# Transposing three quarters of the residual stream with DMA transposes in a two-layer decoder trunk

## The chip, the core and the metric

The kernel runs on one core of a Trainium2 chip. The engines that matter are TensorE (PE for matmuls, PEld for weight loads), VectorE (DVE), ScalarE (ACT) and SyncE (SP), which issues most of the DMAs. Each engine runs its own instruction list in order; semaphores tie the lists together. The metric is the device time of one execution in microseconds (us), as the median of several runs.

## The reference

Two pre-norm layers on a sequence of 256 tokens of width 2048, float32. Each layer has a mixing part (sparse attention and stick-breaking attention) and a SwiGLU part, both added to the residual stream `h`:

```python
def reference(x, positions, ...):
    h = x
    for layer in range(DEPTH):                       # DEPTH = 2
        xn = rms_norm(h, norm_mix[layer])
        h = h + hybrid_mixer(xn, ..., w_in[layer], ..., w_out[layer])
        xn = rms_norm(h, norm_ffn[layer])
        h = h + swiglu(xn, w_gate[layer], w_up[layer], w_down[layer])
    return rms_norm(h, norm_final)

def swiglu(xn, w_gate, w_up, w_down):                # inner width 5632
    return (jax.nn.silu(xn @ w_gate) * (xn @ w_up)) @ w_down
```

## The kernel before

**Precision.** Every large product is done in float32 as three passes of a reduced format: a number is split into `hi` and `lo`, and a product is hi·hi + hi·lo + lo·hi. Activations are split into `xh`/`xl` (or `ah`/`al` inside the SwiGLU part), weights into `hi`/`lo`.

**Weight items.** All weights are streamed in items of 512 KB (2 slices of 128 rows by 512 columns). `load_next` (L155) issues the load on SP into one of 5 `raw` buffers; `split_next` makes `hi` by a copy on ACT (L166) and `lo` by a subtraction on DVE (L167), each in one of 4 buffers; `mm` (L409) then issues 12 matmuls of 512 columns per item: two slices, three passes, two token tiles. `prefetch` keeps the split 3 items ahead of the matmuls and the loads 5 items ahead of the splits. A split can only start when the item four places earlier has released its `hi` buffer.

**Order around the items.** Everything else is written as Python generators. Before each item the main loop does `step(active)`, which advances every generator to its next `yield`, then `prefetch`, then `mm`. So a `yield` is one item of delay, and what a generator emits stands in each engine's list between two splits. The engines do not reorder: an instruction of a generator that waits on ACT holds up the splits behind it.

**Transposing the activations.** Matmuls need the activations with the feature on the partition. The residual stream `h` has the token there. `xt_block` transposes a quarter of `h` (512 features, 2 token tiles) by 8 PE transposes into PSUM (L374, tiles `tps`), multiplies by the norm's gain on DVE (L376, `scr`), copies to `xh` on ACT (L381) and subtracts to `xl` on DVE (L384). `xt_gen` wraps that in a generator. There are three places where `h` is transposed in the steady part: before the SwiGLU part of both layers (during the last column block `o3` of the output projection, items o0 to o3) and before the second layer's mixing part (during the last pass over `w_down`, blocks d0 to d3). Quarter 3 of `h` is final only when the last block is done, so its transposes stand right behind it.

**h_add and d_add** add a finished block to `h` on DVE (L864, L950), and a step later square it on ACT (L347) for the next norm; the last one finishes the norm.

**The gated chain.** Inside the SwiGLU part, `gated` transposes silu(gate)·up, 512 features at a time, without PE: ACT separates the float32 values into two planes of 16-bit halves (`pl`, L923), one DMA transpose moves both planes into `plt` (L926, issued on ACT's queue), ACT interleaves the planes again into `sT` (L934, four instructions), and ACT and DVE split the result into `ah` and `al` (L938, L939). It takes nine steps from the product to `ah`. There are 11 such chunks in each layer, consumed by `w_down` in two groups of 6 and 5 chunks. The first `w_down` block of a group starts right after the group's last chunk is multiplied, and reaches that chunk after 10 items (first group) or 8 items (second).

Of the kernel before, what the change touches and what calls it, by code (L numbers as in the profile page):

```python
# [7 lines left out]
F32 = mybir.dt.float32  # L8
# [114 lines left out]
def trunk(ctx: ExitStack, tc: tile.TileContext, x, positions, cst, gT, gfin, bgate, posT, w2, ws, out):  # L123
# [58 lines left out]
    def spawn(g):  # L182
        active.append(g)
# [204 lines left out]
    def tmp512(name="scr"):  # L388
        return tmpp.tile([P, 512], F32, tag="scr", name=name, bufs=3)

    def xt_gen(X, c, srcs, g, ready=None):
        if ready is not None:
            while ready not in flags:
                yield
        xt_alloc(X, c)
        xt_block(X, c, srcs, g)
        yield
# [43 lines left out]
    for l in range(DEPTH):  # L441
        g_mix, g_grp, g_ffn = gt[:, 3 * l, :], gt[:, 3 * l + 1, :], gt[:, 3 * l + 2, :]
        flags.clear()
        with ExitStack() as actx:
# [357 lines left out]
            def sb_driver(b):  # L802
                yield from wait_for("nsa", f"sq{b}", f"sk{b}")
                yield from pipeline([sb_unit(b, 0, [0, 1, 2, 3]), sb_unit(b, 1, [0, 1]), sb_unit(b, 1, [2, 3])], 2)

            spawn(prep())
            spawn(nsa_driver())
            spawn(sb_driver(0))
# [2 lines left out]

            ocmp = {}
            accs = None
            XO = new_x()
            while seq[pos][1].mat in ("w_in", "w_cmp_k1", "w_cmp_v1"):
                it = seq[pos][1]
                if l == 0 and pos < 6:
# [7 lines left out]
                if it.mat == "w_in":  # L825
                    for kt in it.kts:
                        while X[kt // 4] is None:
                            step(active)
                    if it.first:
                        accs = [acc(), acc()]  # L830
                    mm(pos, accs, lambda kt: X[kt // 4])
                    if it.last:
                        nm = it.name
                        if nm in ("ck", "cv"):
                            spawn(c_chunk(nm, accs))
                        elif nm == "v" or nm[:2] == "sv":
                            spawn(v_chunk(nm, accs))
                        else:
                            spawn(qk_chunk(nm, accs))
                    if it.name == "sv1" and it.kts[-1] in (3, 7, 11):  # L840
                        c = it.kts[-1] // 4
                        spawn(xt_gen(XO, c, lambda t, c=c: on[c][:, t], g_grp, f"on{c}"))
# [33 lines left out]
            while seq[pos][1].mat == "w_out":  # L876
# [5 lines left out]
                if XO[it.kts[0] // 4] is None:  # L882
                    while f"on{it.kts[0] // 4}" not in flags:
                        step(active)
                    need(XO, it.kts[0] // 4)
                    step(active)
                    step(active)
                mm(pos, accs[it.name], lambda kt: XO[kt // 4])
                c = int(it.name[1])
                if it.last:  # L890
                    spawn(h_add(accs[it.name], c, norm))
                if c == 3 and it.kts[-1] in (1, 5, 9, 15):
                    q = it.kts[-1] // 4
                    spawn(xt_gen(X, q, lambda t, q=q: h[:, t, quad(q)], g_ffn, f"h{q}"))
                parts.pop(pos)
                pos += 1

# [1 line left out]
        with ExitStack() as fctx:  # L899
# [14 lines left out]
            def gated(c, accs):  # L914
# [3 lines left out]
                    s = sil[c, t]  # L918
                    V.scalar_tensor_tensor(s, accs[t], r[:, t:t + 1], s, op0=OP.mult, op1=OP.mult)  # L919
                yield  # L920
                pl = fp.tile([P, 2, 2, 512], U16, tag="pl", name="pl", bufs=1)
                for t in range(2):
                    A.activation(pl[:, t], sil[c, t].bitcast(U16).rearrange("p (n b) -> p b n", b=2), AF.Copy)  # L923
                    yield
                pt = fp.tile([P, 2, 2, 512], U16, tag="plt", name="plt", bufs=1)
                nc.scalar.dma_start(pt.rearrange("p t b (a s) -> p (t b a) s", a=4),  # L926
                                    pl.rearrange("p t b n -> p (t b n)"), transpose=True)
                for _ in range(4):
                    yield
                f = fp.tile([P, 4, S], F32, tag="sT", name="sT", bufs=1)  # L930
                fv = f.rearrange("p a s -> p (a s)").bitcast(U16).rearrange("p (a t s b) -> p t b a s", a=4, t=2, b=2)
                for t in range(2):
                    for b in range(2):
                        A.activation(fv[:, t, b], pt[:, t, b].rearrange("p (a s) -> p a s", a=4), AF.Copy)  # L934
                    yield
# [3 lines left out]
                V.tensor_tensor(al, f, ah.bitcast(F32), op=OP.subtract)  # L939
                yield  # L940
                act[c] = (ah, al)

# [37 lines left out]
            while pos < (end_at if last else len(seq)) and seq[pos][1].mat in ("w_gate", "w_up", "w_down"):  # L980
# [10 lines left out]
                if it.last:  # L991
                    c = int(it.name[1:])
                    if it.mat == "w_down":
                        end = it.k1 == KFF
                        spawn(d_add(accs, c, end, norm))
                        if end and not last:
                            spawn(xt_gen(X, c, lambda t, c=c: h[:, t, quad(c)], gt[:, 3 * (l + 1), :], f"d{c}"))
                    else:
                        spawn(silu(c, accs) if it.mat == "w_gate" else gated(c, accs))
                parts.pop(pos)  # L1000
# [95 lines left out]
```

## Time and profile before

| what | value |
|---|---|
| median of 3 runs | 2296.75 us (2296.72 to 2298.61) |
| the profiled execution | 2295.14 us, of it 2293.4 us from its first to its last instruction |
| PE busy | 2269.5 us (99%) |
| DVE busy | 1322.7 us (58%) |
| ACT busy | 1176.6 us (51%) |
| weight loads, queue of SP (q1) | 426.58 MB, 58.4% of the 16 DMA engines |
| DMA transposes, queue of ACT (q10) | 11.54 MB, 3.1% |

Busy time of PE counts each matmul from its start to a modelled end; matmuls overlap, so the starts in the timeline tell what one costs. In the timeline a row is a run of equal instructions: start, time from the first start to the last end, engine, line, operation, tiles, shape, count and, in brackets, the idle time of the engine before it and what ended it.

### The profile page before, as it was taken

The numbers are of one execution on the slowest core, as the hardware profiler recorded it, in microseconds if no ns is written. First come the engines' busy times: TensorE is split into PE (matmuls) and PEld (weight loads), VectorE is DVE, ScalarE is ACT, GpSimd is POOL, SyncE is SP. The second block draws the span as 40 slices with busy tenths as digits, with TensorE's granted clock in tenths as the row PEclk, the third lists the DMA queues.
The fourth block names the chain that finished last, engine by engine and source line by source line (L and its number), as shares of the span: only waits on it lengthen the run. The fifth ranks groups of instructions, "written<-read, shape, count | busy, mean of one in ns | idle before, by whom it ended". The sixth has DMA issues, their size and how long they took to land. (4 is left out here: it accounts for less than half of the span.)

```text
span 2293.4 us, 28108 instructions
## 1 busy us (share of the span) xinstructions
PE 2269.5 (99%) x10666; PEld 1888.1 (82%) x10666; DVE 1322.7 (58%) x1744; ACT 1176.6 (51%) x1515; POOL 28.7 (1%) x59
## 2 busy tenths in 40 slices
PE   8999999999999999999999999999999999999998
PEld 7888888888888888887888888888888888888876
DVE  6766776655545444555567667765545554445554
ACT  6645554555554345555455455545555543455543
POOL 5000000000000000000000000000000000000000
PEclk9999999999999999999999999999999999999999
DMA  7854446567677667776567434456666665566663
GB/s 252 274 174 129 124 153 199 180 204 208 201 208 203 193 193 204 209 203 191 178 215 254 147 129 143 157 186 206 213 197 210 201 203 193 195 209 202 202 193 137
DMA packets 164584, 439.98 MB, mean 192 GB/s; under 512 B 59184, under 2 KB 59600, under 8 KB 164320
## 3 DMA queue, kind: packets, MB, share of 16 engines
q1 hardware_dynamic: 118464, 426.58, 58.4%
q10 hardware_dynamic: 45760, 11.54, 3.1%
q8 instruction: 83, 1.36, 0.2%
q14 instruction: 53, 0.43, 0.1%
q0 software_dynamic: 224, 0.07, 0.0%
HBM read 424.50 MB, written 2.10 MB: 186 GB/s over the span
## 5 line engine op out<-in xcount | busy, mean ns | idle before, releaser
L167 DVE TENSOR_TENSOR lo<-raw,hi 128x1024 fp32r<-128x1024 f32 (+1 forms) x798 | 969.4, 1220 | 829.3 <-ACT hi L166 821.4
L166 ACT ACTIVATE hi<-raw 128x1024 fp32r<-128x1024 f32 (+1 forms) x798 | 835.9, 1054 | 782.4 <-PE acc L409 723.7
L409 PE MATMUL acc<-hi,xh 128*128 128x512 f32 (+2 forms) x2432 | 754.5, 391 | 0.0
L409 PE MATMUL acc<-hi,xl 128*128 128x512 f32 (+2 forms) x2432 | 738.0, 385 | 0.0
L409 PE MATMUL acc<-lo,xh 128*128 128x512 f32 (+2 forms) x2432 | 736.5, 384 | 0.0
L409 PEld LDWEIGHTS acc<-lo,xh 128*128 128x128 f32 x2432 | 452.7, 188 | 92.2 <-DVE lo L167 0.2
L409 PEld LDWEIGHTS acc<-hi,xl 128*128 128x128 f32 x2432 | 452.8, 188 | 91.8
L409 PEld LDWEIGHTS acc<-hi,xh 128*128 128x128 f32 x2432 | 444.7, 188 | 87.0 <-issue 6.7
L409 PE MATMUL acc<-hi,ah 128*128 128x512 f32 x680 | 211.1, 390 | 3.3 <-ACT ah L938 3.3
L409 PE MATMUL acc<-hi,al 128*128 128x512 f32 x680 | 211.0, 389 | 1.4 <-DVE al L939 1.4
L409 PE MATMUL acc<-lo,ah 128*128 128x512 f32 x680 | 210.7, 389 | 0.0
L409 PEld LDWEIGHTS acc<-hi,ah 128*128 128x128 f32 x680 | 127.3, 188 | 30.2 <-ACT ah L938 4.1
L409 PEld LDWEIGHTS acc<-hi,al 128*128 128x128 f32 x680 | 127.5, 188 | 28.7 <-DVE al L939 2.3
L409 PEld LDWEIGHTS acc<-lo,ah 128*128 128x128 f32 x680 | 127.7, 188 | 26.6
L934 ACT ACTIVATE sT<-plt 128x512 uint16<-128x512 uint16 x88 | 61.7, 766 | 0.0
L381 ACT ACTIVATE xh<-scr 128x512 fp32r<-128x512 f32 x48 | 29.2, 630 | 44.3 <-DVE scr L376 44.3
L664 ACT ACTIVATE pT<-tps 128x256 f32<-128x256 f32 (+1 forms) x32 | 15.7, 492 | 63.1 <-PE tps L662 63.1
L923 ACT ACTIVATE pl<-sil 128x1024 uint16<-128x1024 uint16 x44 | 46.2, 1050 | 0.0
L376 DVE TENSOR_TENSOR scr<-tps,gt 128x512 f32<-128x512 f32 x48 | 30.9, 684 | 23.3 <-PE tps L374 23.3
L919 DVE SCALAR_TENSOR_TENSOR sil<-acc,nr,sil 128x512 f32<-128x512 f32 x44 | 31.0, 747 | 13.8 <-PE acc L409 13.8
L910 ACT ACTIVATE sil<-acc,nr 128x512 f32<-128x512 f32 x44 | 27.9, 686 | 15.3 <-PE acc L409 15.3
L384 DVE TENSOR_TENSOR xl<-scr,xh 128x512 fp32r<-128x512 f32 x48 | 31.3, 692 | 5.0 <-ACT xh L381 2.9
(197 smaller groups left out, 978.5 us busy)
## 6 DMA issues: line engine op xcount, KB each, us to landing
raw<-in_ws_dram SPq DMA_DIRECT2D x792, 512.0 KB, 3.9
raw<-in_ws_dram SPq DMA_DIRECT2D x10, 420.0 KB, 5.0
h<-in_x_dram SPq DMA_DIRECT2D x3, 512.0 KB, 8.4
gf<-in_gfin_dram SPq DMA_DIRECT2D x1, 1024.0 KB, 7.2
out_dram<-h SPq DMA_DIRECT2D x4, 256.0 KB, 2.2
out_dram<-h SPq DMA_DIRECT2D x2, 512.0 KB, 3.1
cs<-in_cst_dram SPq DMA_DIRECT2D x1, 802.0 KB, 5.8
h<-in_x_dram SPq DMA_DIRECT2D x2, 256.0 KB, 4.0
```

Of the source, the lines that this page charges most:

```text
L166: A.activation(hi[:, :n], r[:, :n], AF.Copy)
L167: V.tensor_tensor(lo[:, :n], r[:, :n], hi[:, :n].bitcast(F32), op=OP.subtract)
L376: V.tensor_tensor(tv, pt.rearrange("p (a b) -> p a b", a=4), g[:, 4 * c:4 * c + 4, None].to_broadcast([P, 4, P]), op=OP.mult)
L381: A.activation(xh[:, :, t * P:t * P + P], ts[t], AF.Copy)
L384: V.tensor_tensor(xl[:, :, sl], ts[t], xh[:, :, sl].bitcast(F32), op=OP.subtract)
L409: T.matmul(accs[t][:, :it.w], x_[:, kt % 4, t * P:t * P + P], w_[:, sl], start=(kt == it.k0 and n == 0), stop=(kt == it.k1 - 1 and n == 2))
L664: A.activation(w[:, :nb * P], pt[:, :nb * P], AF.Copy)
L910: A.activation(s, accs[t], AF.Silu, scale=r[:, t:t + 1])
L919: V.scalar_tensor_tensor(s, accs[t], r[:, t:t + 1], s, op0=OP.mult, op1=OP.mult)
L923: A.activation(pl[:, t], sil[c, t].bitcast(U16).rearrange("p (n b) -> p b n", b=2), AF.Copy)
L934: A.activation(fv[:, t, b], pt[:, t, b].rearrange("p (a s) -> p a s", a=4), AF.Copy)
```

## The change

A generator `flip` holds the DMA transpose that `gated` had: two `pl` copies in one step, the DMA transpose on SP's queue instead of ACT's, three steps of delay, then two interleaving copies instead of four (each token tile at once, written contiguously, read alternately from the two planes). A list `turn` lets one flip run at a time. `gated` uses it; from the product to `ah` it takes five steps. `flip_x` uses it for quarters 0 to 2 of `h` in all three places: gain on DVE over the whole quarter (128x1024), `xh` and `xl` in one instruction each. Quarter 3 stays with `xt_gen`. In the output projection the flips start with the first item of o2; quarters 1 and 2 wait for buffers that o3 releases (`gone0`, `gone1`). The scratch space for software DMAs is set to 4096.

```diff
+    def flip(srcs, dst, steps=3):
+        while turn:
+            yield
+        turn.append(dst)
+        pl = tmpp.tile([P, 2, 2, 512], U16, tag="pl", name="pl", bufs=1)
+        for t in range(2):
+            A.activation(pl[:, t], srcs(t).bitcast(U16).rearrange("p (n b) -> p b n", b=2), AF.Copy)
+        pt = tmpp.tile([P, 2, 2, 512], U16, tag="plt", name="plt", bufs=1)
+        nc.sync.dma_start(pt.rearrange("p t b (a s) -> p (t b a) s", a=4),
+                          pl.rearrange("p t b n -> p (t b n)"), transpose=True)
+        for _ in range(steps):
+            yield
+        fv = dst().bitcast(U16).rearrange("p (a t s b) -> p t a s b", a=4, t=2, b=2)
+        for t in range(2):
+            A.activation(fv[:, t], pt[:, t].rearrange("p b (a s) -> p a s b", a=4), AF.Copy)
+        yield
+        turn.pop()
+
+    def flip_x(X, c, srcs, g, ready, slot=None):
+        while ready not in flags:
+            yield
...
+        yield from flip(srcs, dst)
+        turn.append(f)
+        fv = f[0].rearrange("p (a s) -> p a s", a=4)
+        V.tensor_tensor(fv, fv, g[:, 4 * c:4 * c + 4, None].to_broadcast([P, 4, S]), op=OP.mult)
+        while (slot is not None and slot not in flags) or (c and X[c - 1] is None):
+            yield
+        xt_alloc(X, c)
+        xh, xl = X[c]
+        A.activation(xh, fv, AF.Copy)
+        V.tensor_tensor(xl, fv, xh.bitcast(F32), op=OP.subtract)
+        turn.pop()
+        yield
...
+                c = int(it.name[1])
+                if c == 2 and it.first:
+                    for q in range(3):
+                        spawn(flip_x(X, q, lambda t, q=q: h[:, t, quad(q)], g_ffn, f"h{q}",
+                                     f"gone{q - 1}" if q else None))
                 mm(pos, accs[it.name], lambda kt: XO[kt // 4])
-                c = int(it.name[1])
                 if it.last:
                     spawn(h_add(accs[it.name], c, norm))
-                if c == 3 and it.kts[-1] in (1, 5, 9, 15):
-                    q = it.kts[-1] // 4
-                    spawn(xt_gen(X, q, lambda t, q=q: h[:, t, quad(q)], g_ffn, f"h{q}"))
+                if c == 3 and it.kts[-1] % 4 == 3:
+                    flags.add(f"gone{it.kts[-1] // 4}")
+                if c == 3 and it.last:
+                    spawn(xt_gen(X, 3, lambda t: h[:, t, quad(3)], g_ffn, "h3"))
...
-                pl = fp.tile([P, 2, 2, 512], U16, tag="pl", name="pl", bufs=1)
-                for t in range(2):
-                    A.activation(pl[:, t], sil[c, t].bitcast(U16).rearrange("p (n b) -> p b n", b=2), AF.Copy)
-                    yield
-                pt = fp.tile([P, 2, 2, 512], U16, tag="plt", name="plt", bufs=1)
-                nc.scalar.dma_start(pt.rearrange("p t b (a s) -> p (t b a) s", a=4),
-                                    pl.rearrange("p t b n -> p (t b n)"), transpose=True)
-                for _ in range(4):
-                    yield
...
-                for t in range(2):
-                    for b in range(2):
-                        A.activation(fv[:, t, b], pt[:, t, b].rearrange("p (a s) -> p a s", a=4), AF.Copy)
-                    yield
...
+                yield from flip(lambda t: sil[c, t], dst)
...
-                            spawn(xt_gen(X, c, lambda t, c=c: h[:, t, quad(c)], gt[:, 3 * (l + 1), :], f"d{c}"))
+                            spawn((flip_x if c < 3 else xt_gen)(X, c, lambda t, c=c: h[:, t, quad(c)],
+                                                                gt[:, 3 * (l + 1), :], f"d{c}"))
...
-    nc = _bacc.Bacc("TRN2", target_bir_lowering=False, num_devices=1)
+    nc = _bacc.Bacc("TRN2", target_bir_lowering=False, num_devices=1, dynamic_dma_scratch_size=4096)
```

How the instructions now stand, at three places. In the names `hi`, `lo`, `xh`, `xl` are the splits told of above, `sT` the transposed quarter, `scr` the product with the gain (or the scratch of a square), `nss` and `nr` parts of the norm; the number is the buffer's.

ACT, first layer, from o3 to the first SwiGLU items. Before, each of quarters 1 and 2 has two copies to `xh` between the weight splits, and then come the squares of quarter 3:

```order
L381 ACTIVATE xh_3809<-scr_3816 128x4x128
L381 ACTIVATE xh_3809<-scr_3823 128x4x128
L166 ACTIVATE hi_3829<-raw_3696 128x1024
L166 ACTIVATE hi_3847<-raw_3714 128x1024
L381 ACTIVATE xh_3865<-scr_3872 128x4x128
L381 ACTIVATE xh_3865<-scr_3879 128x4x128
L166 ACTIVATE hi_3885<-raw_3734 128x1024
L166 ACTIVATE hi_3903<-raw_3777 128x1024
L166 ACTIVATE hi_3921<-raw_3795 128x1024
L166 ACTIVATE hi_3947<-raw_3833 128x1024
L347 ACTIVATE scr_3967,nss_3187<-h_82 128x512 x2
```

Now, the same stretch from quarter 1's interleaving copies to quarter 2's `xh`:

```order
L409 ACTIVATE sT_3746<-plt_3690 128x4x256 x2
L166 ACTIVATE hi_3751<-raw_3647 128x1024
L347 ACTIVATE scr_3772,nss_3187<-h_82 128x512 x2
L166 ACTIVATE hi_3775<-raw_3668 128x1024
L431 ACTIVATE xh_3793<-sT_3746 128x1024
L401 ACTIVATE pl_3797<-h_82 128x1024 x2
L166 ACTIVATE hi_3802<-raw_3696 128x1024
L166 ACTIVATE hi_3820<-raw_3714 128x1024
L166 ACTIVATE hi_3838<-raw_3732 128x1024
L409 ACTIVATE sT_3856<-plt_3800 128x4x256 x2
L166 ACTIVATE hi_3859<-raw_3755 128x1024
L431 ACTIVATE xh_3878<-sT_3856 128x1024
```

A quarter's DMA transpose is now enclosed in ACT's list: `pl` of the next quarter stands right behind `xh` of the one before, and three splits stand between `pl` and `sT`.

DVE at the end of the same stretch, where the last block is added to `h` (L864 before, L909 now), which PE's transposes of quarter 3 read. Before:

```order
L384 TENSOR_TENSOR xl_3866<-scr_3872,xh_3865 128x4x128
L384 TENSOR_TENSOR xl_3866<-scr_3879,xh_3865 128x4x128
L167 TENSOR_TENSOR lo_3886<-raw_3734,hi_3885 128x1024
L167 TENSOR_TENSOR lo_3904<-raw_3777,hi_3903 128x1024
L167 TENSOR_TENSOR lo_3922<-raw_3795,hi_3921 128x1024
L864 TENSOR_TENSOR h_82<-h_82,acc_3736 128x512
L864 TENSOR_TENSOR h_82<-h_82,acc_3737 128x512
```

Now:

```order
L167 TENSOR_TENSOR lo_3860<-raw_3755,hi_3859 128x1024
L426 TENSOR_TENSOR sT_3856<-sT_3856,gt_77 128x1024
L432 TENSOR_TENSOR xl_3879<-sT_3856,xh_3878 128x1024
L167 TENSOR_TENSOR lo_3883<-raw_3779,hi_3882 128x1024
L167 TENSOR_TENSOR lo_3901<-raw_3806,hi_3900 128x1024
L909 TENSOR_TENSOR h_82<-h_82,acc_3757 128x512
L909 TENSOR_TENSOR h_82<-h_82,acc_3758 128x512
```

Between the work on quarter 2 and the two additions there were three splits of weights; now there are two.

ACT in the gated chain of the second chunk, from `pl` to `ah`. Before:

```order
L923 ACTIVATE pl_4611<-sil_4437 128x1024
L166 ACTIVATE hi_4632<-raw_4539 128x1024
L926 DMA_TRANSPOSE plt_4650<-pl_4611 128x16x128
L166 ACTIVATE hi_4652<-raw_4557 128x1024
L166 ACTIVATE hi_4670<-raw_4575 128x1024
L166 ACTIVATE hi_4688<-raw_4595 128x1024
L166 ACTIVATE hi_4706<-raw_4617 128x1024
L934 ACTIVATE sT_4724<-plt_4650 128x4x128 x2
L166 ACTIVATE hi_4727<-raw_4636 128x1024
L934 ACTIVATE sT_4724<-plt_4650 128x4x128 x2
```

Now:

```order
L401 ACTIVATE pl_4588<-sil_4416 128x1024
L401 ACTIVATE pl_4588<-sil_4418 128x1024
L166 ACTIVATE hi_4593<-raw_4498 128x1024
L166 ACTIVATE hi_4611<-raw_4516 128x1024
L166 ACTIVATE hi_4629<-raw_4534 128x1024
L409 ACTIVATE sT_4647<-plt_4591 128x4x256 x2
L166 ACTIVATE hi_4650<-raw_4552 128x1024
L982 ACTIVATE ah_4668<-sT_4647 128x1024
```

Three splits stand between `pl` and the interleaving copies, where there were four between the DMA's issue and them; `ah` follows one split later.

## Rows read from the trace of the kernel before

**Rows 1.** Page: busy line, granted clock by slice; groups by line: transposes of `h`.

```profile
PE 2269.5 (99%) x10666; PEld 1888.1 (82%) x10666; DVE 1322.7 (58%) x1744; ACT 1176.6 (51%) x1515; POOL 28.7 (1%) x59
...
PEclk9999999999999999999999999999999999999999
...
L374 PE MATMUL tps<-cs,h 128*128 128x128 f32 x128 | 20.0, 303 | 9.8 <-DMA cs<-in_cst_dram 4.1 <-DMA h<-in_x_dram 3.4 <-DVE scr L376 1.7
```

**Rows 2.** Timeline of PE: two items of o2 and o3, one with transposes.

```profile
399.19 0.62 PE L409 MATMUL acc<-hi,xh 128*128 128x512 f32 x2
399.64 0.62 PE L409 MATMUL acc<-hi,xl 128*128 128x512 f32 x2
...
401.91 0.62 PE L409 MATMUL acc<-hi,xh 128*128 128x512 f32 x2
...
404.64 1.03 PE L374 MATMUL tps<-cs,h 128*128 128x128 f32 x8
405.43 0.71 PE L409 MATMUL acc<-hi,xh 128*128 128x512 f32 x2
...
408.24 0.62 PE L409 MATMUL acc<-hi,xh 128*128 128x512 f32 x2
```

**Rows 3.** Timeline of PE: second group's first `w_down` block, first and second layer.

```profile
1057.87 0.61 PE L409 MATMUL acc<-lo,ah 128*128 128x512 f32 x2
1060.12 0.73 PE L409 MATMUL acc<-hi,ah 128*128 128x512 f32 x2 [1.64 <-ACT ah L938]
1061.58 0.73 PE L409 MATMUL acc<-hi,al 128*128 128x512 f32 x2 [0.72 <-DVE al L939]
...
1064.00 0.61 PE L409 MATMUL acc<-hi,ah 128*128 128x512 f32 x2
...
2193.89 0.61 PE L409 MATMUL acc<-lo,ah 128*128 128x512 f32 x2
2196.14 0.73 PE L409 MATMUL acc<-hi,ah 128*128 128x512 f32 x2 [1.64 <-ACT ah L938]
...
2200.03 0.62 PE L409 MATMUL acc<-hi,ah 128*128 128x512 f32 x2
```

**Rows 4.** Timeline of ACT in o2 and o3, first layer.

```profile
398.94 1.06 ACT L166 ACTIVATE hi<-raw 128x1024 fp32r<-128x1024 f32 x1 [1.66 <-PE acc L409]
401.66 1.06 ACT L166 ACTIVATE hi<-raw 128x1024 fp32r<-128x1024 f32 x1 [1.66 <-PE acc L409]
402.62 0.61 ACT L347 ACTIVATE scr<-h 128x512 f32<-128x512 f32 x1
...
403.90 0.18 ACT L347 ACTIVATION_READ_ACCUMULATOR scr<-h 128x1 f32 x1
...
407.13 2.00 ACT L166 ACTIVATE hi<-raw 128x1024 fp32r<-128x1024 f32 x2
```

**Rows 5.** Timeline of DVE, same stretch.

```profile
400.03 1.23 DVE L167 TENSOR_TENSOR lo<-raw,hi 128x1024 fp32r<-128x1024 f32 x1 [1.49 <-ACT hi L166]
401.88 1.29 DVE L864 TENSOR_TENSOR h<-h,acc 128x512 f32<-128x512 f32 x2 [0.63 <-PE acc L409]
...
408.21 2.36 DVE L167 TENSOR_TENSOR lo<-raw,hi 128x1024 fp32r<-128x1024 f32 x2 [0.25 <-ACT hi L166]
```

**Rows 6.** The DMA transpose (issue time on ACT's queue) and its landing, by source line.

```profile
L926 ACTq DMA_TRANSPOSE plt<-pl x22: 1333/3644/4919, 476.1 to 2177.8; - x22
...
DMA to landing us min/median/max: 5.3/7.4/9.6
```

**Rows 7.** Page: copies around the DMA transpose; below, timeline of ACT in one chunk.

```profile
L934 ACT ACTIVATE sT<-plt 128x512 uint16<-128x512 uint16 x88 | 61.7, 766 | 0.0
L381 ACT ACTIVATE xh<-scr 128x512 fp32r<-128x512 f32 x48 | 29.2, 630 | 44.3 <-DVE scr L376 44.3
L923 ACT ACTIVATE pl<-sil 128x1024 uint16<-128x1024 uint16 x44 | 46.2, 1050 | 0.0
...
2189.61 1.41 ACT L934 ACTIVATE sT<-plt 128x512 uint16<-128x512 uint16 x2
```

**Rows 8.** DMA queues (packets, MB, share); issues (count, KB, landing); waits of SP's queue.

```profile
q1 hardware_dynamic: 118464, 426.58, 58.4%
q10 hardware_dynamic: 45760, 11.54, 3.1%
...
raw<-in_ws_dram SPq DMA_DIRECT2D x792, 512.0 KB, 3.9
...
SPq L155 <- DVE lo L167: 1707.5, 732, 8.2
```

**Rows 9.** Timeline of ACT at the first block of the last `w_down` pass, first layer.

```profile
1067.54 1.28 ACT L955 ACT_TABLE_LOAD   x1
```

More of the change, by code (lines that the diff above doesn't have):

```diff
@@ L389, in tmp512, with dst @@
         return tmpp.tile([P, 512], F32, tag="scr", name=name, bufs=3)
+    turn = []
+    def flip(srcs, dst, steps=3):
[18 more added lines that the diff above has]
+            yield
+        f = []
+        def dst():
+            f.append(tmpp.tile([P, 1024], F32, tag="sT", name="sT", bufs=1))
+            return f[0]
+        yield from flip(srcs, dst)
[10 more added lines that the diff above has]
+        yield
     def xt_gen(X, c, srcs, g, ready=None):
-        if ready is not None:
-            while ready not in flags:
-                yield
+        while (ready is not None and ready not in flags) or (c and X[c - 1] is None):
+            yield
         xt_alloc(X, c)
@@ L804, in sb_driver @@
                 yield from pipeline([sb_unit(b, 0, [0, 1, 2, 3]), sb_unit(b, 1, [0, 1]), sb_unit(b, 1, [2, 3])], 2)
+            XO = new_x()
             spawn(prep())
@@ L813, in trunk @@
             accs = None
-            XO = new_x()
             while seq[pos][1].mat in ("w_in", "w_cmp_k1", "w_cmp_v1"):
@@ L839, in trunk @@
                             spawn(qk_chunk(nm, accs))
-                    if it.name == "sv1" and it.kts[-1] in (3, 7, 11):
-                        c = it.kts[-1] // 4
-                        spawn(xt_gen(XO, c, lambda t, c=c: on[c][:, t], g_grp, f"on{c}"))
+                    if it.name == "sv1":
+                        if it.kts[-1] in (3, 7, 11):
+                            c = it.kts[-1] // 4
+                            spawn(xt_gen(XO, c, lambda t, c=c: on[c][:, t], g_grp, f"on{c}"))
                 else:
@@ L920, in gated, with dst @@
                 yield
-                pl = fp.tile([P, 2, 2, 512], U16, tag="pl", name="pl", bufs=1)
-                for t in range(2):
-                    A.activation(pl[:, t], sil[c, t].bitcast(U16).rearrange("p (n b) -> p b n", b=2), AF.Copy)
-                    yield
-                pt = fp.tile([P, 2, 2, 512], U16, tag="plt", name="plt", bufs=1)
-                nc.scalar.dma_start(pt.rearrange("p t b (a s) -> p (t b a) s", a=4),
-                                    pl.rearrange("p t b n -> p (t b n)"), transpose=True)
-                for _ in range(4):
-                    yield
-                f = fp.tile([P, 4, S], F32, tag="sT", name="sT", bufs=1)
-                fv = f.rearrange("p a s -> p (a s)").bitcast(U16).rearrange("p (a t s b) -> p t b a s", a=4, t=2, b=2)
-                for t in range(2):
-                    for b in range(2):
-                        A.activation(fv[:, t, b], pt[:, t, b].rearrange("p (a s) -> p a s", a=4), AF.Copy)
-                    yield
+                f = []
+                def dst():
+                    f.append(tmpp.tile([P, 1024], F32, tag="sT", name="sT", bufs=1))
+                    return f[0]
+                yield from flip(lambda t: sil[c, t], dst)
+                turn.append(f)
+                f = f[0].rearrange("p (a s) -> p a s", a=4)
                 ah = fp.tile([P, 4, S], F32R, tag="ah", name="ah", bufs=6)
@@ L939, in gated @@
                 V.tensor_tensor(al, f, ah.bitcast(F32), op=OP.subtract)
+                turn.pop()
                 yield
```

## Prediction

> **What bounds the kernel now.** I read the page first: PE is busy 99% of the span at full granted clock [rows 1], so only what shortens PE's list or fills its few gaps can help. The busy figure must not be used as a price: by the groups, a transpose of `h` has a mean of 303 ns, and 72 of them would be 21.8 us. The timeline of PE says what they cost. An item of 12 matmuls takes 401.91 - 399.19 = 2.72 us from start to start; the next two items with 8 transposes between them take 408.24 - 401.91 = 6.33 us, so the 8 transposes cost 6.33 - 5.44 = 0.89 us [rows 2]. Third, the gaps: in each layer the first block of the second `w_down` group waits for `ah` and `al` [rows 3]. Fourth, ACT and DVE: in a plain item ACT copies `hi` for 1.06 us and then waits for PE [rows 4], DVE subtracts for 1.23 us [rows 5]. They have time, but they run only three items ahead of PE and in fixed order. So I ask of every added step how long it holds up the splits behind it.
>
> **The change part by part.**
>
> *PE transposes.* Three places lose three quarters each: 9 groups of 8, 9 x 0.89 = 8.0 us. PE's list has nothing else to do in that time, so all of it counts.
>
> *The shorter gated chain.* From 1057.87 to 1064.00 there are 7 pairs of matmuls, which need 7 x 2.72 / 6 = 3.17 us and took 6.13: 2.96 lost. In the second layer 2200.03 - 2193.89 = 6.14: 2.97 lost [rows 3]. Now `ah` comes four items earlier, which is more than 10 us, so both gaps go: 5.9 us. Together 13.9 us to be had.
>
> *What is added to ACT's list.* A flip is two `pl` copies, the DMA transpose, its landing, and two interleaving copies, with three weight splits between. If the landing is late, ACT stands still, and the splits behind it with it. Call the time from issue to landing L and the two interleaving copies c. The trace of before has 22 such transposes: L was 5.3 at least, 7.4 in the median, 9.6 at most [rows 6]. For c the nearest rows are the `pl` copies, 1050 ns for 1024 values of 16 bits, a pair 2.0 us with the overlap that two `hi` copies show (2.00), and the old four interleaving copies, 1.41 us for two, so 2.8 us for four [rows 4, 7]. I take 2.0: the new copies have the size of `pl` and write contiguously as it does, while the old ones wrote every other 16-bit value. The old ones need 766 ns for 512 values where a float32 copy of 512 needs 630 [rows 7], so c could be 2.8.
>
> [...]
>
> *For L I take 5.3.* The old transposes were sent while weight loads came every 2.72 us on another queue. Each of some 800 loads takes 58.4% x 2293.4 / 800 = 1.7 us of all 16 DMA engines, a transpose 3.1% x 2293.4 / 22 = 3.2 us [rows 8]; with two loads beside it, 7.4 is no surprise. Now the transpose stands in the same list as the loads. In the output projection it is issued about 2 us behind a load, and the next load stands behind it, so it meets less traffic: the shortest old landing is the nearest. Both ends stay for the range.
>
> [...]
>
> *The chain in the output projection.* Three flips follow each other there within two blocks. Time zero is the start of the `hi` copy ahead of the first `pl`. It lies 0.25 us before an item's first matmul (401.66 and 401.91) [rows 2, 4]. Then, all in series:
> - `hi` and the squares of the block before: 402.62 to 404.08, so `pl` starts at 2.4 [rows 4];
> - each flip: `pl` pair 2.0, hand-overs 0.15 (an estimate; `hi` to `lo` takes 0.03 [rows 4, 5]), L, c: 2.15 + L + c, three times;
> - from one flip's end to the next `pl`: `hi` 1.06, `lo` 1.23, gain on DVE 1.13, `xh` 0.95, about 4.4, twice. The DVE step is taken from a pair of subtractions, 2.36 for two [rows 5]; the squares of another block fit beside it on ACT;
> - from the last flip's end to the additions to `h`: `hi` 1.06, `lo` 1.23, gain 1.13, `xh` 1.06, `xl` 1.13, two more `lo` 2.26, the two additions 1.29: 9.2 [rows 4, 5].
>
> Sum: 2.4 + 6.45 + 8.8 + 9.2 = 26.9, plus 3 (L + c). PE comes to the transposes of quarter 3, which need those additions, after 17 items: 0.25 + 17 x 2.72 = 46.5. It then waits 3 (L + c) - 19.6. With L + c = 7.3 that is 2.3 us per layer, 4.6 us in all. On the way the splits are in time: the closest, the `lo` behind the third `pl`, is done at 34.4, its item starts at 35.6. When L + c is larger they come late first, but as the chain is serial the total stays the same formula.
>
> *The other flips are covered.* At the end of the first layer they are 10 items apart. The worst has a table load of 1.28 us in front [rows 9]: the split behind its `xh` is done at 2.4 + 1.3 + 9.45 + 4.4 + 2.3 = 19.9, its item starts at 0.25 + 8 x 2.72 = 22.0. In the gated chain the split behind the interleaving copies is done at 1.0 + 9.45 + 2.3 = 12.8, its item starts at 0.25 + 7 x 2.72 = 19.3; even the longest landing (4.3 later) fits.
>
> *SP's queue.* The issue of a transpose took 1.3 to 4.9 us on ACT [rows 6], now it holds up the loads behind it, and its data another 3.2: at most 8.1 us. A load is issued when `lo` has freed its buffer, 2.4 us after the `hi` copy, lands 3.9 later [rows 8], and is needed five items on, at 13.6: 7.3 us to spare, and behind that the three items that the splits are ahead. Most of the time SP waits for `lo` (1707.5 us) [rows 8]. I cost it at nothing. That ACT no longer issues transposes hides in ACT's waiting. The scratch size and the earlier XO list move nothing on PE.
>
> Sum on the profiled execution: 2295.14 - 8.0 - 5.9 + 4.6 = 2285.8; the median of the runs lies 1.6 above that execution, so 2287.4 us.
>
> **The rivals.**
> - *All of it hidden.* If L + c is 6.5 or less, no wait remains: 2296.75 - 13.9 = 2282.8. It needs a landing of 4.5, below every one seen. Chance 0.10.
> - *The landing stays at its median.* L = 7.4 and c = 2.0: 3 x 9.4 - 19.6 = 8.6 per layer, 17.2 in all, +3.3: 2300.0, no change that can be told. For it: it is the median of 22 landings, and loads flow as before; against it: the gap between loads where the flips stand. Chance 0.23 for L + c from 8.1 to 9.6. [...]
> - *Slower: the transpose waits for its turn among the loads.* On SP the transpose queues behind the loads' packets, so that it lands like the latest of before: L = 9.6, 15.2 per layer, 2296.75 - 13.9 + 30.4 = 2313.2. It decides from L + c = 9.6 on (L = 7.6), where the two waits pass 18.5 us and the time passes 2301.3. For it: a fixed order in one queue; against it: at each such issue at most one load is on its way. Chance 0.14.
> - The forecast, L + c from 6.5 to 8.1, 2282.8 to 2292.2: chance 0.53.
>
> **How the numbers follow.** Less than 0.2% (4.6 us) can hardly be told from no change. Faster: forecast and first rival, 0.63. Same: 0.23. Slower: 0.14. The range goes from the first rival, 2282, through the second to the beginning of the third, 2302; that leaves out some 0.15, nearly all above.
>
> **What would show it.** 31 DMA transposes on SP and none on ACT; 56 transposes of `h` on PE instead of 128; no wait for `ah`; before the transposes of quarter 3 in the SwiGLU's first item a wait of PE for the additions, some 2 us in each layer, and none in the gated chunks. The interleaving copies should take about 1.05 us each, the landings in the output projection about 5.3. I am wrong if the landings are at 7 or more, if the copies take 1.4, if `hi` splits in the gated chunks become late, or if PE waits for weights.

## The result, and the profile after

The changed kernel takes 2283.64 us (median of 4 runs, 2282.37 to 2285.54) against 2297.61 us of the kernel before on the same chip (4 runs, 2296.72 to 2298.61). The ratio is 0.9941, with an interval of 0.9929 to 0.9953: faster by 14 us, and inside the predicted range (2282 to 2302). From here on numbers are spans of the profiled executions, since the steps can be added there: 2293.4 us before, 2281.2 us after, 12.2 us less.

The page of the changed kernel, busy line, granted clock, DMA queue, the interleaving copies and the issues (columns as in [rows 1, 7, 8]):

```profile
PE 2261.2 (99%) x10594; PEld 1881.0 (82%) x10594; DVE 1319.5 (58%) x1726; ACT 1197.2 (52%) x1498; POOL 28.7 (1%) x59
...
PEclk9999999999999999999999999999999999999999
...
q1 hardware_dynamic: 182944, 442.84, 62.5%
...
L409 ACT ACTIVATE sT<-plt 128x1024 uint16<-128x1024 uint16 x62 | 69.7, 1172 | 19.0 <-DMA plt<-pl 18.9
...
raw<-in_ws_dram SPq DMA_DIRECT2D x792, 512.0 KB, 4.0
```

PE has 72 instructions fewer (10666 in [rows 1]), which are the nine groups of eight transposes. ACT's queue for DMAs is gone, SP's carries the transposes too. From 20 us after the start to the first flip, PE's matmuls start 0.12 to 0.16 us earlier than before throughout, so neither the scratch size nor the earlier XO list that the prediction names moves anything there. ACT stood 18.9 us waiting for a DMA transpose ahead of its copies; what of that reached PE is the question.

The timeline of PE, changed kernel, at the end of the output projection and in the first SwiGLU item, first layer, then second:

```profile
423.54 0.62 PE L453 MATMUL acc<-hi,xh 128*128 128x512 f32 x2
...
427.85 1.26 PE L374 MATMUL tps<-cs,h 128*128 128x128 f32 x8 [1.43 <-DVE h L909]
428.86 0.70 PE L453 MATMUL acc<-hi,xh 128*128 128x512 f32 x2
...
1553.02 0.62 PE L453 MATMUL acc<-hi,xh 128*128 128x512 f32 x2
...
1555.74 1.23 PE L374 MATMUL tps<-cs,h 128*128 128x128 f32 x8
1556.72 0.70 PE L453 MATMUL acc<-hi,xh 128*128 128x512 f32 x2
```

The same place before, first layer:

```profile
426.39 0.62 PE L409 MATMUL acc<-hi,xh 128*128 128x512 f32 x2
...
429.12 1.03 PE L374 MATMUL tps<-cs,h 128*128 128x128 f32 x8
429.91 0.71 PE L409 MATMUL acc<-hi,xh 128*128 128x512 f32 x2
```

The item that holds the transposes of quarter 3 takes 428.86 - 423.54 = 5.32 us in the first layer and 1556.72 - 1553.02 = 3.70 in the second. An item takes 2.72, and with these transposes it took 429.91 - 426.39 = 3.52 before, 0.80 more. So PE waits 1.80 us and 0.18 us for the additions to `h`: 2.0 in all. From the first item of o2 on to the end of a layer PE has one other wait for an engine or a DMA, 0.55 us for the additions of d3 in the first layer, and that one is as long in the kernel before. The waits for `ah` and `al` of [rows 3] are gone, and every item of o2, o3 and the `w_down` blocks that had one of the nine groups beside it now takes 2.72.

The sum by rows: nine groups 9 x 0.89 = 8.0, two waits for `ah` and `al` 5.9, new waits 2.0: 11.9 us less, where the spans differ by 12.2.

The same stretch on ACT, changed kernel, is the chain of the three flips:

```profile
379.76 1.06 ACT L166 ACTIVATE hi<-raw 128x1024 fp32r<-128x1024 f32 x1 [1.66 <-PE acc L453]
...
382.10 1.99 ACT L401 ACTIVATE pl<-h 128x1024 uint16<-128x1024 uint16 x2
...
390.43 2.25 ACT L409 ACTIVATE sT<-plt 128x1024 uint16<-128x1024 uint16 x2 [1.44 <-DMA plt<-pl]
...
397.08 1.99 ACT L401 ACTIVATE pl<-h 128x1024 uint16<-128x1024 uint16 x2
398.97 2.94 ACT L166 ACTIVATE hi<-raw 128x1024 fp32r<-128x1024 f32 x3
403.47 2.26 ACT L409 ACTIVATE sT<-plt 128x1024 uint16<-128x1024 uint16 x2 [1.56 <-DMA plt<-pl]
...
410.13 1.99 ACT L401 ACTIVATE pl<-h 128x1024 uint16<-128x1024 uint16 x2
...
416.91 2.26 ACT L409 ACTIVATE sT<-plt 128x1024 uint16<-128x1024 uint16 x2 [1.95 <-DMA plt<-pl]
```

And its end on DVE:

```profile
423.70 1.23 DVE L432 TENSOR_TENSOR xl<-sT,xh 128x1024 fp32r<-128x1024 f32 x1 [1.19 <-ACT xh L431]
424.84 2.35 DVE L167 TENSOR_TENSOR lo<-raw,hi 128x1024 fp32r<-128x1024 f32 x2
427.11 1.28 DVE L909 TENSOR_TENSOR h<-h,acc 128x512 f32<-128x512 f32 x2
```

Each flip ends in a wait of ACT for the DMA (1.44, 1.56, 1.95); the three splits between hide most of the landing, not all. The wait of PE in the first layer follows the sum of the three landings one for one in the four runs that have the same chain: landings of 14.86, 15.27, 15.29 and 15.48 us (third, first and second profile of the changed kernel, and the flips of `h` alone, below) go with waits of 1.39, 1.80, 1.81 and 2.03. The landings of these flips, by source line in the changed kernel (first the three of the first layer, then of the second, then the eleven gated chunks of the first layer; count, issue time in ns as least, median and most):

```profile
L403 SPq DMA_TRANSPOSE plt<-pl x3: 1949/2836/2861, 384.1 to 412.1; - x3
...
DMA to landing us min/median/max: 4.3/4.7/6.3
...
L403 SPq DMA_TRANSPOSE plt<-pl x3: 1406/1773/1856, 1513.6 to 1540.4; - x3
...
DMA to landing us min/median/max: 4.3/4.6/4.7
...
L403 SPq DMA_TRANSPOSE plt<-pl x11: 3430/3634/4543, 472.7 to 1038.5; - x11
...
DMA to landing us min/median/max: 5.6/6.6/7.3
```

### The profile page after: what moved, and what is told of

Its sections match the earlier page's. It is cut to its first block, busy times and chain, and to the rows that moved or that the text cites. A ratio compares the mean times of both kernels' runs of the same rounds, so it can differ in the third digit from the quotient of the medians.

```text
span 2281.2 us, 27958 instructions
## 1 busy us (share of the span) xinstructions
PE 2261.2 (99%) x10594; PEld 1881.0 (82%) x10594; DVE 1319.5 (58%) x1726; ACT 1197.2 (52%) x1498; POOL 28.7 (1%) x59
## 4 chain that ended last, share of the span: by engine, by line
PE 95%; ACT 2%; DVE 2%; DMA 1%; issue 1%; SPq 0%; ACTq 0%; DVEq 0%
PE acc L453 88%; PE ops L714 1%; PE tps L685 1%; PE ops L583 1%; DMA plt<-pl 1%; PE ops L584 1%; PE tps L660 1%; DVE lo L167 1%; PE tps L706 0%; ACT hi L166 0%; DMA raw<-in_ws_dram 0%; PE tps L374 0%; DVE c L817 0%; PE ops L841 0%; PE tps L808 0%
## 5 line engine op out<-in xcount | busy, mean ns | idle before, releaser
L409 ACT ACTIVATE sT<-plt 128x1024 uint16<-128x1024 uint16 x62 | 69.7, 1172 | 19.0 <-DMA plt<-pl 18.9
L401 ACT ACTIVATE pl<-sil 128x1024 uint16<-128x1024 uint16 x44 | 44.1, 1050 | 0.0
L583 PE MATMUL ops<-hi,fr 128*60 128x256 f32 x128 | 31.7, 281 | 0.0
L584 PE MATMUL ops<-lo,fr 128*60 128x256 f32 x128 | 31.4, 279 | 0.0
L347 ACT ACTIVATE scr<-h 128x512 f32<-128x512 f32 x38 | 23.8, 626 | 13.2 <-DVE h L995 9.7
```

Source lines behind the costliest of these rows:

```text
L347: A.activation(scr, h[:, t, quad(c)], AF.Square, accum_out=self.ss[:, t, c:c + 1])
L401: A.activation(pl[:, t], srcs(t).bitcast(U16).rearrange("p (n b) -> p b n", b=2), AF.Copy)
L409: A.activation(fv[:, t], pt[:, t].rearrange("p b (a s) -> p a s b", a=4), AF.Copy)
L583: T.matmul(o[:60, :256], fr[:, kt, :], hi[:, sl], start=(kt == 0), stop=False)
L584: T.matmul(o[:60, :256], fr[:, kt, :], lo[:, sl], start=False, stop=(kt == 31))
```

## The experiments

The theory: the gain is 8.0 us of transposes and 5.9 us of waits, less what three flips in series put before PE's transposes of quarter 3; that price follows the landing L, the interleaving copies c and the start of the first flip. The main rival: where the transpose is issued decides, because on SP it queues differently with the loads than it did on ACT. All kernels with their spans:

| kernel | median us | ratio to before (interval) | span us |
|---|---|---|---|
| changed (two more times) | 2283.37; 2283.31 | 0.9938 (0.9926 to 0.9951); 0.9942 (0.9928 to 0.9955) | 2281.0; 2281.1 |
| gated chain alone | 2289.55 | 0.9966 (0.9954 to 0.9979) | 2287.5 |
| flips of `h` alone | 2290.94 | 0.9972 (0.9961 to 0.9983) | 2289.4 |
| issued on ACT | 2286.93 | 0.9957 (0.9941 to 0.9972) | 2285.4 |
| early start (two times) | 2281.42; 2281.55 | 0.9933 (0.9921 to 0.9946); 0.9931 (0.9919 to 0.9943) | 2279.6; 2279.9 |
| four interleaving copies | 2284.99 | 0.9947 (0.9932 to 0.9962) | 2282.9 |
| quarter 3 flipped too | 2292.63 | 0.9980 (0.9971 to 0.9989) | 2291.1 |
| an extra transpose ahead | 2303.75 | 1.0029 (1.0018 to 1.0040) | 2302.1 |

### The two halves apart

The gated chain alone: `h` is transposed on PE everywhere, by the old calls of `xt_gen`.

```diff
-                if c == 2 and it.first:
-                    for q in range(3):
-                        spawn(flip_x(X, q, ..., f"gone{q - 1}" if q else None))
...
+                if c == 3 and it.kts[-1] in (1, 5, 9, 15):
+                    q = it.kts[-1] // 4
+                    spawn(xt_gen(X, q, lambda t, q=q: h[:, t, quad(q)], g_ffn, f"h{q}"))
...
-                            spawn((flip_x if c < 3 else xt_gen)(X, c, ...))
+                            spawn(xt_gen(X, c, ...))
```

> Only the gated chain is changed (flip on the sync queue, two copies each, five steps); all quarters of h are transposed on PE as before, with their 72 transposes. Theory (the gains add: 8.0 us of PE transposes, 5.9 us of waits for ah, less the wait before quarter 3): both waits for ah are gone and nothing else moves, span 2293.4 - 5.9 = 2287.5 us. Rival (the shorter chain only moves the wait, to a late hi or to a later chunk): span 2291 or more, with new PE gaps in the SwiGLU part.

Measured: 2287.5, which is 2293.4 - 5.9 to the tenth, and PE's waits for `ah` and `al` are gone. The shorter chain alone gives the whole of its term, and no new wait of PE appears.

The flips of `h` alone: the gated chunks get back the delays that the old chain had.

```diff
-    def flip(srcs, dst, steps=3):
+    def flip(srcs, dst, steps=3, slow=False):
...
+            if slow:
+                yield
...
-                yield from flip(lambda t: sil[c, t], dst)
+                yield from flip(lambda t: sil[c, t], dst, 4, True)
```

> Three quarters of h are flipped as in the changed kernel, but the gated chain keeps its old delays (pl in two steps, four steps to the first interleaving copy, nine in all), on the sync queue. Theory: PE loses 9 x 0.89 = 8.0 us of transposes, gets the waits before quarter 3 (1.8 us in the first layer, 0.2 in the second), and keeps the two waits for ah of 2.96 us: span 2293.4 - 8.0 + 2.0 = 2287.4 us. With the run of the gated chain alone the two gains sum to 11.9, the changed kernel's span fell by 12.2. Rival (the transposes on PE were worth less, since PE also hid other waits): span above 2289.

Measured: 2289.4, 2.0 more than expected. The new waits are those of the changed kernel (2.03 and 0.03 us), the first layer's wait for `ah` is the old one, 2.94. In the second layer waits of the same length were followed by something new. Its timeline of PE, and the windows of PE there (length; busy and count; granted clock; DMA share; GB/s):

```profile
2190.62 0.73 PE L458 MATMUL acc<-hi,ah 128*128 128x512 f32 x2 [1.64 <-ACT ah L987]
2192.08 0.77 PE L458 MATMUL acc<-hi,al 128*128 128x512 f32 x2 [0.72 <-DVE al L988]
2192.65 1.05 PE L458 MATMUL acc<-lo,ah 128*128 128x512 f32 x2
...
2196.05 0.63 PE L458 MATMUL acc<-hi,ah 128*128 128x512 f32 x2
```

```profile
2192.00:2194.00 2.00, 1.92 (x6) 0.66 0.67 244
2194.00:2196.00 2.00, 2.00 (x6) 0.50 0.00 0
```

The granted clock falls to 0.50 for about 3.4 us. In it four pairs of matmuls take 2196.05 - 2192.65 = 3.40 us, where four take 4 x 0.453 = 1.81 at full clock: 1.6 lost. The other 0.5 us lies ahead of the output projection, where this kernel is that much later. By its span alone the rival of this run (above 2289) would stand, but each of the nine items that lost its transposes is shorter by the full 0.8 to 0.9 us. So the mechanism held: 5.9 + 4.0 us for the two halves, with the 1.6 of the clock and the 0.5 of the start, make 12.0 of the 12.2 us of the changed kernel. The waits before the fall, 1.64 and 0.72 us, are those of the kernel before [rows 3], whose clock stayed at 1.00 there in both layers (1058 to 1065 us and 2194 to 2200 us); in the first layer of this run the same two cost 2.94 us, no more than the 2.96 of before.

### The queue

The DMA transpose is issued by ACT again, nothing else is changed.

```diff
-        nc.sync.dma_start(pt.rearrange("p t b (a s) -> p (t b a) s", a=4),
+        nc.scalar.dma_start(pt.rearrange("p t b (a s) -> p (t b a) s", a=4),
```

> The changed kernel with its DMA transposes issued on ACT's queue instead of SP's, nothing else. Theory A (the landing in the output projection is short, 4.3 to 6.3, because the transposes stand in a gap between loads, whichever queue issues them): landings there stay at about 5, the wait before quarter 3 at about 2 us over both layers, span within 1.5 us of 2281.2; only in the gated chunks do the landings return to about 7. Theory B (it is short because the next load stands behind the transpose in the same queue and cannot compete): landings return to 7.4 everywhere; 3 x 2.4 more per layer, so about 7 us of waits more in each layer, span about 2295.

Measured: 2285.4, between the two. The landings in the output projection, by source line, in the first layer and below it in the second, and ACT's timeline at the third flip:

```profile
L403 ACTq DMA_TRANSPOSE plt<-pl x3: 1547/1952/3366, 384.4 to 412.1; - x3
...
DMA to landing us min/median/max: 4.3/5.2/5.3
...
DMA to landing us min/median/max: 4.3/4.6/5.2
```

```profile
412.08 3.37 ACTq L403 DMA_TRANSPOSE plt<-pl  x1
415.49 2.95 ACT L166 ACTIVATE hi<-raw 128x1024 fp32r<-128x1024 f32 x3 [3.44 <-issue]
418.35 2.24 ACT L409 ACTIVATE sT<-plt 128x1024 uint16<-128x1024 uint16 x2
```

The landing is the same on either queue, 28.9 us for the six together in both kernels, so the rival falls: short landings belong to the place in the program, not to SP's list. Over all 31 transposes, too, the landings are alike: 4.3 to 7.7 us on SP, 5.6 in the median, and 4.3 to 8.2 on ACT, 5.5 in the median. What makes the place short is not shown by a run of its own. The rows fit the loads beside the transpose: the load ahead of the second flip in the first layer had landed 0.7 us before the transpose was issued, while in the gated chunks a load is issued 0.4 us before it (472.32 and 472.71 us on SP for the first). What SP gives is the issue time: on ACT the splits behind the transpose stand for 3.44 us, start when most of the landing is over (it takes at most 5.3 us from 412.08) and end behind it, at 418.44, so they come late. By the lengths of its items PE waits 2.84 us and 3.03 us in the two layers, for late splits and for the additions, instead of 1.8 and 0.2: 3.9 of the 4.2 us by which the span is longer.

So the issue of the third flip in the first layer, 3.37 us, is not small beside a landing of at most 5.3, and issuing on ACT cost those 3.9 us of waiting.

### The start, the copies and the landing

Each flip of the output projection starts as soon as its block is done.

```diff
-                if c == 2 and it.first:
-                    for q in range(3):
-                        spawn(flip_x(X, q, ..., f"gone{q - 1}" if q else None))
...
                 if it.last:
                     spawn(h_add(accs[it.name], c, norm))
+                    if c < 3:
+                        spawn(flip_x(X, c, ..., f"gone{c - 1}" if c else None))
```

> The changed kernel, but each flip in the output projection is started when its block is done (flip of quarter 0 after o0) instead of with the first item of o2, so the first two flips stand two items earlier. Theory (one serial chain of three flips ends in the additions that PE's transposes of quarter 3 wait for): the chain then begins 5.4 us earlier up to the third flip, which waits for a buffer that o3 releases; from there on 3.0 + 2.15 + 4.7 + 2.25 + 9.2 us lead to the additions, no later than PE. Both waits go, 2.0 us: span 2279.2. Rival (the wait is set by the third flip alone, or by the additions themselves): the waits of 1.8 and 0.2 us remain and the span is 2281.2.

Measured: 2279.6. In the first layer the transposes of quarter 3 now follow the last matmuls almost at once, and in the second at once (timeline of PE, early start):

```profile
425.94 0.61 PE L453 MATMUL acc<-lo,xh 128*128 128x512 f32 x2
426.56 1.25 PE L374 MATMUL tps<-cs,h 128*128 128x128 f32 x8
...
1554.45 1.03 PE L374 MATMUL tps<-cs,h 128*128 128x128 f32 x8
```

Of 2.0 us of waiting 0.4 remain, and the span is 1.6 us shorter. The first `pl` starts 382.10 - 376.80 = 5.3 us earlier, but the squares behind the additions only 427.83 - 426.53 = 1.3. ACT's timeline, early start, between the second flip and the third:

```profile
397.15 2.25 ACT L409 ACTIVATE sT<-plt 128x1024 uint16<-128x1024 uint16 x2 [1.70 <-DVE lo L167]
...
407.56 1.06 ACT L431 ACTIVATE xh<-sT 128x1024 fp32r<-128x1024 f32 x1 [0.61 <-PE acc L453]
408.52 1.99 ACT L401 ACTIVATE pl<-h 128x1024 uint16<-128x1024 uint16 x2
```

The `xh` of quarter 1 needs a buffer that o3 releases (`gone0`), so it stands later in ACT's list and waits 0.61 us for PE besides: from the second flip's end to the third `pl` pass 9.1 us instead of 4.4. That gives back most of the earlier start. Both kernels ran again beside each other on one chip.

> The early start once more, beside the changed kernel on one chip, in more rounds, to tell the two apart. My theory (three flips in series, whose end sets PE's wait before the transposes of quarter 3): an early start takes away the 2.0 us that are left of the two waits, less some 0.4, so its span is 1.4 to 2.0 us below that of the changed kernel, some 2279.6 against 2281.2, and the median of the runs is lower by about as much. Rival: the two waits are not on the path that sets the end, what is saved there is given back later (splits that come late behind the earlier flips), and the spans agree within 0.5 us.

> The changed kernel a third time, as the partner of the early start in the same job. Both theories: span 2281.0 to 2281.2 as in its two other profiles; waits of PE before the transposes of quarter 3 of about 1.8 us in the first layer and 0.2 us in the second.

Measured: 2281.55 us (2280.98 to 2281.65) against 2283.31 us (2282.85 to 2285.32), 5 runs each, which do not overlap; spans 2279.9 and 2281.1. The early start beats both kernels. Its lead in the spans is 1.2 us, less than expected, because the changed kernel waited 1.39 and 0.12 us here and not 1.8 and 0.2: the landings of its first layer sum to 14.86 us in place of 15.27. The other run of the changed kernel, whose span was 2281.0, says the same of the waits as the first (1.81 and 0.03 us):

> The changed kernel once more, on the chip of this comparison, for the medians: ratio 0.994 to the kernel before, landings of the six flips in the output projections between 4.2 and 6.5 us, waits before quarter 3 of 1 to 2 us in the first layer and 0 to 1 in the second, as they follow the landings.

Then c: the interleaving by the old four copies, which write every other 16-bit value.

```diff
-        fv = dst().bitcast(U16).rearrange("p (a t s b) -> p t a s b", a=4, t=2, b=2)
+        fv = dst().bitcast(U16).rearrange("p (a t s b) -> p t b a s", a=4, t=2, b=2)
         for t in range(2):
-            A.activation(fv[:, t], pt[:, t].rearrange("p b (a s) -> p a s b", a=4), AF.Copy)
+            for b in range(2):
+                A.activation(fv[:, t, b], pt[:, t, b].rearrange("p (a s) -> p a s", a=4), AF.Copy)
```

> The changed kernel, but planes are interleaved by four copies of 512 values each as before (1.41 us for two) instead of two copies of 1024 (2.25 us for the pair): c goes from 2.25 to 2.82. Theory (serial chain, three flips per layer): 3 x 0.57 = 1.7 us more of wait before quarter 3 in each layer, 3.5 in the first and 1.9 in the second, nothing in the gated chunks: span 2281.2 + 3.4 = 2284.6 us. Rival (ACT has time enough, the wait is set by landings alone): span stays at 2281.2.

Measured: 2282.9, 1.7 above the changed kernel, half of what was expected. ACT's timeline at the first flip, and the wait of PE in the first layer:

```profile
390.43 2.66 ACT L410 ACTIVATE sT<-plt 128x512 uint16<-128x512 uint16 x4 [1.16 <-DMA plt<-pl]
```

```profile
428.71 1.25 PE L374 MATMUL tps<-cs,h 128*128 128x128 f32 x8 [2.00 <-DVE h L910]
```

Four copies take 2.66 us, two take 2.25: 0.41 each flip, 1.2 us a layer by the formula. The six landings were together 0.9 us shorter in this run, so 1.6 us is due for both layers, and PE's waits grew by 0.6 and 0.9 us. The slope is right; c was expected to differ by more.

Then L: an unused transpose of the same planes is issued ahead of each flip of `h`, so that the one that counts lands later.

```diff
...
+        if twice:
+            p2 = tmpp.tile([P, 1024], F32, tag="sT", name="sT", bufs=1)
+            nc.sync.dma_start(p2.bitcast(U16).rearrange("p (k s) -> p k s", s=P),
+                              pl.rearrange("p t b n -> p (t b n)"), transpose=True)
...
-        yield from flip(srcs, dst)
+        yield from flip(srcs, dst, twice=True)
```

> The changed kernel with a second, unused DMA transpose of the same planes issued ahead of each of the nine flips of h, which only lengthens the time to the landing, by an estimated 2.4 us (the data of one transpose). Theory (three landings in series per output projection): the wait before quarter 3 and late splits together grow by 3 x 2.4 = 7.2 us in each layer; span about 2281.2 + 14 = 2295 us, at the three flips of the first layer's end at most 1 us. Rival (landings overlap with other work, and the wait comes from the copies on ACT): less than 3 us more.

Measured: 2302.1, 20.9 above the changed kernel and well above what was expected. From the first issue to the second landing passed 8.4, 6.8 and 8.6 us in the first layer and 7.0, 8.3 and 7.1 in the second. That is 23.7 and 22.4 against 15.3 and 13.6 in the changed kernel: 17.2 us more, or 2.9 per flip. The 2.4 us that had been taken for it were an estimate and stand in no row. The rest is mostly the clock. PE's timeline and windows, extra transpose:

```profile
428.81 0.87 PE L457 MATMUL acc<-hi,xh 128*128 128x512 f32 x2 [2.16 <-ACT hi L166]
...
436.48 1.97 PE L374 MATMUL tps<-cs,h 128*128 128x128 f32 x8 [3.06 <-DVE h L913]
...
1574.45 1.97 PE L374 MATMUL tps<-cs,h 128*128 128x128 f32 x8 [4.30 <-DVE h L913]
```

```profile
437.00:438.00 1.00, 1.00 (x6) 0.50 0.87 307
...
1576.00:1578.00 2.00, 2.00 (x7) 0.50 1.01 363
```

The delay now shows in the splits too: PE waits 2.16 us for `hi`, then 3.06 for `h`. As predicted, a larger L makes splits late first and the total still grows by three times L. Behind the last wait of each layer the granted clock is 0.50; the transposes and items there take 1.3 and 2.2 us longer than at full clock, which is most of the remaining 20.9 - 17.2 = 3.7 us. So a longer landing costs what the formula behind the slower rival says, and the clock on top. That a transpose waits behind loads, which is the rival's reason for a long landing, this run does not show.

### Quarter 3 as well

The early start, with quarter 3 of the output projection flipped too, so that no PE transposes remain there. The edit, against the early start:

```diff
-                    if c < 3:
+                    if c <= 3:
                         spawn(flip_x(X, c, ..., f"gone{c - 1}" if c else None))
...
-                if c == 3 and it.last:
-                    spawn(xt_gen(X, 3, lambda t: h[:, t, quad(3)], g_ffn, "h3"))
```

> The kernel with the early start, but quarter 3 in the output projection is flipped as well, so PE loses 16 more transposes of h (2 x 0.9 us) and the wait before them (0.4 us in the first layer). Theory (the flip of the last quarter is longer than the six items before its use): additions end 3.5 us after the last item of o3, then squares and norm 2.5, pl 2.0, landing 4.8, copies 2.25, hi, lo and gain 3.4, xh 1.1: some 19.5 us against 6 x 2.72 = 16.3; PE waits 3 to 4 us per layer at the seventh SwiGLU item: span 2279.6 - 2.2 + 7 = 2284 us. Rival (the flip is hidden): 2277.4 us.

Measured: 2291.1, 11.5 more than the early start and more than expected. PE's timeline in the first SwiGLU items and its windows in the second layer:

```profile
443.45 1.22 PE L453 MATMUL acc<-hi,xh 128*128 128x512 f32 x2 [3.27 <-ACT xh L431]
...
1577.23 1.22 PE L453 MATMUL acc<-hi,xh 128*128 128x512 f32 x2 [4.97 <-ACT xh L431]
```

```profile
1580.00:1582.00 2.00, 2.00 (x6) 0.50 0.70 244
```

From the last additions (425.86 in the first layer) to the end of quarter 3's `xh` (443.40) pass 17.5 us, since the squares, the end of the norm and a whole flip (landing 5.7, in the second layer 8.1) stand in that chain, and PE has only 440.18 - 425.86 = 14.3 us of items (to the start of the 3.27 us of waiting) before it needs quarter 3. The two waits and the lower clock behind them cost 5.3 us and 8.3 us more than whole items take; 2 x 0.8 us of transposes and the 0.4 us of waiting that the early start has left are saved: 13.6 - 2.0 = 11.6. So stopping at three of four quarters is right in this kernel: the fourth has no work of PE long enough to hide its flip. The expectation had waits of 3 to 4 us where 3.27 and 4.97 came, and nothing for the clock.

## Why the prediction was right, step by step

- *PE transposes, 8.0 us.* Right. Nine groups are gone and the items beside them take 2.72. The mean of 303 ns per transpose in [rows 1] would have promised 21.8.
- *The gated chain, 5.9 us.* Right to the tenth in the kernel with that half alone. No split in the gated chunks came late, though landings there went to 7.7.
- *The chain of three flips.* Right in its links: from `hi` to `pl` 2.34 us (2.4), from a flip's end to the next `pl` 4.40 and 4.40 (4.4), from the last flip's end to the end of the additions 9.22 (9.2). The slope of one for each flip's L and c is borne out by the four copies, the extra transpose and the four runs with the same chain.
- *Its size, 4.6 us of waiting, was the mis-sized term: it is 2.0.* Three things make it up. L was taken as 5.3, the shortest landing of [rows 6]; five of the six landings were 4.3 to 4.7 and one 6.3, 28.9 us in all instead of 31.8, so 2.9 less. c was taken as 2.0 and is 2.25, 1.5 more in six flips. And the working let PE wait for both additions, while its first four transposes need only the first token tile: they start about 0.6 us before the end of the additions, 1.2 less in two layers. 4.6 - 2.9 + 1.5 - 1.2 = 2.0, as measured. The three partly cancel, which is luck: the landings alone would have put the sum 2.9 us off.
- *The reason for L* was half right. That the transpose stands in the same list as the loads does not shorten it, as the run on ACT shows (28.9 us for the six on either queue). Less traffic beside it fits most of the rows, but no run changed the traffic alone. The first landing of 6.3 does not fit: it had one load in flight, as the third with 4.7 had. It is no chance, since the two other profiles of the changed kernel have 6.4 and 6.2 there; why it takes longer stays open.
- *Copies.* A copy takes 1160 to 1192 ns (1172 in the mean), not the 1050 of `pl`, so 12% more. Both write contiguously; `pl` reads every other value, this copy alternately from two planes, and no run separates that from other causes.
- *The other flips and SP's queue, nothing.* Right. Loads land in 4.0 us (3.9 in [rows 8]) with transposes of up to 4.5 us of issue ahead of them, and PE waits for none.
- *The rivals.* "All of it hidden" needs L + c of 6.5; the mean was 28.9 / 6 + 2.25 = 7.1. The measured median, 2283.6, lies nearer to this rival's 2282.8 than to the forecast's 2287.4, so the time alone does not tell the two apart; the 2.0 us of waiting does. "The landing stays at its median" fails on the landings: with 7.4 the six would sum to 44.4 us, not 28.9. The time of "slower" appears when the landing is forced up.

The sum gave a gain of 9.3 us, and the spans show 12.2; 2.6 of the difference are that one term.

## What to carry to other kernels

When a DMA takes over work from the busiest engine, find the place where several such transfers follow each other in series, write down the chain link by link up to the first instruction of the busy engine that needs its end, and keep the transfer's landing as a variable: each microsecond of it counts once per transfer in the chain. Take the landing from rows at the same place in the program: here it was 4.3 to 6.3 us in the output projections and 5.1 to 7.7 in the gated chunks, while the queue made no difference to the sum. Issue it from an engine that has nothing urgent behind it (here SP in place of ACT took 4.2 us off the span), and start the first one as early as its data allows (1.2 to 1.6 us here).

## What had not been expected of the hardware

- A wait of PE can cost more than its length: in three of these kernels the granted clock was 0.50 for 3 to 6 us behind a wait, and the one such stretch in the flips alone cost 1.6 us. The waits were 2.16, 3.06, 3.27, 4.30 and 4.97 us, and at the last four of these the clock had fallen before PE went on. Once it fell behind two waits of 1.64 and 0.72, which in the kernel before left it at 1.00, and a single one of 2.00 us in the run with four copies did not slow the transposes behind it (1.25 us, and 1.26 in the changed kernel, where the clock was 1.00). What decides is not settled here.
- A DMA transpose of 512 KB from one tile to another landed in 4.3 us at best and 9.6 at most, and its issue alone held the queue for 1.3 to 4.6 us on SP and 1.3 to 4.9 on ACT.
